# The gate and up products of a second feed-forward as seven half-size products per tile

## The chip, the cores and the metric

The kernel runs on one core of a Trainium2 chip. The metric is the device time of one execution in microseconds, the median of several runs. TensorE (PE) multiplies, VectorE (DVE), ScalarE (ACT) and GpSimd (POOL) work element by element, SyncE (SP) issues the loads; each runs its own list of instructions in order and waits for the others by semaphores.

## What is computed

One hybrid decoder layer on 512 tokens of width 1024: feed-forward, token mixing, feed-forward, each with a normalization ahead and behind and a shift, a scale and a gate from a conditioning vector. The change lies in the second feed-forward. Cut to that, the reference is

```python
def swiglu(y, w_gate, w_up, w_down):
    return (jax.nn.silu(y @ w_gate) * (y @ w_up)) @ w_down

y = rmsnorm(h, ffn2_pre_g[l]) * (1.0 + sc3) + sh3
y = swiglu(y, ffn2_w_gate[l], ffn2_w_up[l], ffn2_w_down[l])
h = h + FFN_RESIDUAL_WEIGHT * g3 * rmsnorm(y, ffn2_post_g[l])
```

with y of 512 x 1024, gate and up weights of 1024 x 2816 and down weights of 2816 x 1024, all float32.

## The kernel before

**Precision.** Every float32 operand is split into a float32r part (`hi`, a cast) and the rest (`lo`, a subtraction). A product of two operands is three matmuls in one accumulator (`mm3`, lines 110 to 113): hi by hi, then the two mixed ones. Each matmul loads its own 128 x 128 weights.

**Units.** `unit` (line 95) loads 128 x 1024 float32 (512 KB) on SP's queue into one of four raw buffers (tag `raw`), casts it on ACT (line 106) and subtracts on DVE (line 107). The results take turns in four `hi` and four `lo` buffers. A raw buffer is free again when the subtraction has read it. The names are `r_`, `h_` and `l_` for raw, hi and lo, with `b` for the second feed-forward, `a` for the first, `db` for the down weights of the second.

**Gate and up.** The 2816 columns are 22 tiles of 128. Tokens are the moving columns, so the result of a tile, 128 x 512, stands transposed in one PSUM bank for the gate and one for the up product. The first three tiles (`FF2_F`) are computed in two halves of 256 tokens, the first half of all three ahead of the second halves, because the tokens of `y` arrive in four tiles of 128 (`y_token_tile`, lines 189 to 213, with a cast and the subtraction `ylo` at line 212). The weights of f = 2 are split into a part of the tiles `hThi2` and `hTlo2` that is not yet in use. The other 19 tiles go through `up_tile`: two units, 48 matmuls of 512 columns, then `swiglu_evac` (lines 216 to 222): a sigmoid on ACT, two multiplications on DVE, the cast into `hThi2` on ACT and the subtraction into `hTlo2` on DVE.

**Rest.** Behind each of the first tiles one step of `rest` is popped: eight `ada(2, 2, j)`, each a 512 KB load and multiply-reductions on DVE (line 132) for the gate of the residual, then `gate_rows` and `gate_load`.

**Down.** `down` runs two halves of 512 output columns with 11 units each; a unit has 24 matmuls of 512 columns with `hThi2` and `hTlo2` as weights.

**Order.** The source gives the work in program order; a scheduler then sets each engine's list, and the pools of buffers decide which buffer a load takes. The `GAP` constants leave unused bytes between groups of buffers.

Of the kernel before, what the change touches and what calls it, by code (L numbers as in the profile page):

```python
# [19 lines left out]
FF = 2816  # L20
NF = FF // P
NH = 4
EPS = 1e-6
START_F = 3
GAP_W = 160
GAP_Y = 64
GAP_H = 128
GAP_M = 64
FF2_F = 3

# [2 lines left out]
def layer_kernel(ctx: ExitStack, tc: tile.TileContext, x, c, cols, gate_b,  # L33
                 ident_d, masks_d, causal_d, ada_w, wgu1, wd1, w_ft, w_vh, w_mv, w_out, wgu2, wd2, out):
    nc = tc.nc
# [19 lines left out]
    def mm_tile(name):  # L55
        return psum.tile([P, 512], F32, tag="mm", name=name)
# [4 lines left out]
    def tmp_tile(name):  # L61
        return tmp.tile([P, D], F32, tag="tmp", name=name)
# [126 lines left out]
    def y_token_tile(s, i, y, n):  # L189

        ts_ = slice(i * P, (i + 1) * P)
        for q in range(2):
# [31 lines left out]
    def k3(u):
        return tuple(v.rearrange("p (k n) -> p k n", k=KT) for v in u)
# [7 lines left out]
                    k == 0, k == KT - 1)  # L233
        swiglu_evac(f, ps[0], ps[1], hT, tag)

    def down(wd, hT, tag, s, nxt, n=NF, order=lambda f: f, pump=None, drain=None, rest=()):


        t0, ss0, later = [], [], []
        nu = n // 2  # L240
        for half in range(2):
            acc = [mm_tile(f"pd{tag}_{half}_{i}") for i in range(NT)]

            def step(u, i, v):
                for e in range(2):
                    f = order(2 * u + e)
                    mm3(acc[i], (hT[0][:, f, i * P:(i + 1) * P], hT[1][:, f, i * P:(i + 1) * P]),
                        (v[0][:, e, :], v[1][:, e, :]), u == 0 and e == 0, u == nu - 1 and e == 1)

            last = []  # L250
            for u in range(nu):
                v = unit(wd[half, u], 1024, f"d{tag}_{half}_{u}")
                v = tuple(a.rearrange("p (e n) -> p e n", e=2) for a in v)
                if rest:
                    rest.pop(0)()
                if u < nu - 4 or (drain and half == 0):
                    if drain and u == nu - 1:
                        drain()
                    for i in range(NT):
                        step(u, i, v)  # L260
                        if pump:
                            pump()
                else:
                    last.append((u, v))
            for i in range(NT):
                for n_, (u, v) in enumerate(last):
                    step(u, i, v)
                    if n_ == 0 and len(later) > 1:
                        later.pop(0)()
                if half == 0:  # L270
                    yt = small.tile([P, T], F32, tag="ysb", name=f"ysb{tag}_{i}", bufs=4)
                    ss = small.tile([P, 1], F32, tag="ssa", name=f"ssa{tag}_{i}", bufs=4)
                    nc.scalar.activation(yt, acc[i], AF.Square, accum_out=ss)
                    nc.vector.tensor_tensor(out=yt, in0=acc[i], in1=gates[s][:, 0:T], op=ALU.mult)
                    t0.append(yt)
                    ss0.append(ss)
                    continue
                post(tag, s, i, t0[i], acc[i], ss0[i], nxt is None)
                if nxt is not None:
                    nn = normed(i, nxt[0])  # L280
# [515 lines left out]


    def ffn2(y, later):
        with tc.tile_pool(name="hT2", bufs=1) as hp:
            phase(hp, "gap_h2", GAP_H)  # L800
            hT = (hp.tile([P, NF, T], F32R, name="hThi2"), hp.tile([P, NF, T], F32R, name="hTlo2"))
            us = []
            for f in range(FF2_F):
                us.append([])
                for g in range(2):
                    dst = None
                    if f == FF2_F - 1:
                        sl = slice(NF - 2 * (g + 1), NF - 2 * g)
                        dst = tuple(a[:, sl, :].rearrange("p a b -> p (a b)") for a in hT)
                    us[f].append(k3(unit(wgu2[f, g], 1024, f"b_{f}_{g}", dst)))  # L810
            ps = []
            for hf in range(2):
                sl = slice(hf * 256, (hf + 1) * 256)
                for f in range(FF2_F):
                    if hf == 0:
                        ps.append([mm_tile(f"pub_{f}_{g}") for g in range(2)])
                    for g in range(2):
                        for k in range(KT):
                            mm3(ps[f][g][:, sl], (us[f][g][0][:, k, :], us[f][g][1][:, k, :]),
                                (y[0][:, k, sl], y[1][:, k, sl]), k == 0, k == KT - 1)  # L820
                            if later and k == 3 and f == g:
                                later.pop(0)()
# [85 lines left out]
```

## Time and profile before

| what | value |
|---|---|
| median of 3 runs | 1053.97 us (1053.57 to 1054.98) |
| the profiled execution's own time | 1054.96 us |
| its span | 1053.2 us |
| mean granted clock of TensorE | 0.997 |
| gate and up, first three tiles | about 680 to 717 us |
| gate and up, 19 whole tiles | 718 to 927 us |
| down of the second feed-forward | 927 to 1045 us |

A span is the time from the first to the last instruction of the profiled execution. Busy times are sums per engine; a table by stretches shows which engine is full in which stage. A wait is named by what released it. The landing of a load is counted from its issue.

### The profile page before, as it was taken

How to read it: one execution, taken by the hardware profiler on the slowest of the kernel's cores; microseconds unless marked ns; L12 is line 12 of the kernel's file. 1: busy time of each engine (PE TensorE's matmuls, PEld its weight loads, DVE VectorE, ACT ScalarE, POOL GpSimd, SP SyncE). 2: the span in 40 equal slices, each digit the busy share in tenths (PEclk: the TensorE clock that was granted, in tenths of full speed). 3: DMA queues.
4: the chain of work that ended last, by engine and by line, in shares of the span. 5: the costliest groups of instructions: out<-in, count | busy, mean ns of one | idle time of the engine just before them, and what ended most of it. 6: DMA issues, size and time to landing. Idle time of an engine off the chain costs nothing.

```text
span 1053.2 us, 13118 instructions
## 1 busy us (share of the span) xinstructions
PE 1031.8 (98%) x4988; PEld 857.2 (81%) x4988; DVE 600.4 (57%) x1426; ACT 344.8 (33%) x496; POOL 70.7 (7%) x104
## 2 busy tenths in 40 slices
PE   6999999999999999999999999999999999999997
PEld 4778888888888878978888887898888888888886
DVE  7975465566555285387879775775543433332323
ACT  5542233222212164435343223632322222221311
POOL 1000000000000020022223131100000000000000
PEclk9999999999999999999999999999999999999999
DMA  9864445555655413333223311144454223322212
GB/s 343 279 212 152 147 153 156 164 158 165 197 180 166 149 63 126 107 124 111 100 81 100 101 61 61 44 153 146 138 111 149 92 89 101 100 99 81 100 40 80
DMA packets 42938, 136.39 MB, mean 130 GB/s; under 512 B 7670, under 2 KB 8054, under 8 KB 42876
## 3 DMA queue, kind: packets, MB, share of 16 engines
q1 hardware_dynamic: 42588, 135.41, 39.7%
q8 instruction: 39, 0.64, 0.2%
q10 hardware_dynamic: 288, 0.16, 0.1%
q14 instruction: 23, 0.19, 0.1%
HBM read 133.43 MB, written 2.12 MB: 129 GB/s over the span
## 4 chain that ended last, share of the span: by engine, by line
PE 86%; DVE 8%; issue 1%; DMA 1%; POOL 1%; ACT 1%; DVEq 0%; POOLq 0%; SPq 0%; ACTq 0%
PE pub L111 7%; PE pub L113 7%; PE pub L112 7%; PE pua L112 7%; PE pua L111 7%; PE pua L113 7%; PE pft L113 4%; PE pft L112 4%; PE pft L111 4%; PE pdb L112 4%; PE pdb L111 4%; PE pdb L113 4%; PE pda L111 4%; PE pda L113 3%; PE pda L112 3%; PE pl L576 3%
## 5 line engine op out<-in xcount | busy, mean ns | idle before, releaser
L111 PE MATMUL pub<-yhi,h_b 128*128 128x512 f32 (+1 forms) x368 | 137.8, 375 | 0.0
L113 PE MATMUL pub<-yhi,l_b 128*128 128x512 f32 (+1 forms) x368 | 137.0, 372 | 0.0
L112 PE MATMUL pub<-ylo,h_b 128*128 128x512 f32 (+1 forms) x368 | 136.0, 370 | 0.0
L111 PE MATMUL pua<-yhi,h_a 128*128 128x512 f32 x304 | 119.3, 392 | 0.7 <-DVE ta L219 0.7
L112 PE MATMUL pua<-ylo,h_a 128*128 128x512 f32 x304 | 119.8, 394 | 0.0
L113 PE MATMUL pua<-yhi,l_a 128*128 128x512 f32 x304 | 118.0, 388 | 0.0
L106 ACT CAST h_b<-r_b 128x1024 fp32r<-128x1024 f32 x42 | 44.0, 1051 | 137.8 <-issue 102.3
L107 DVE TENSOR_TENSOR l_b<-r_b,h_b 128x1024 fp32r<-128x1024 f32 x42 | 51.3, 1224 | 60.3 <-ACT h_b L106 60.3
L132 DVE CUSTOM_DVE_ANT_0 a<-a,sc 128x256 f32<-128x256 f32 x216 | 82.4, 425 | 0.0
L113 PEld LDWEIGHTS pub<-yhi,l_b 128*128 128x128 f32 x368 | 69.1, 188 | 13.4
L111 PE MATMUL pft<-yhi,h_ft 128*128 128x512 f32 x192 | 79.6, 415 | 0.0
L112 PEld LDWEIGHTS pub<-ylo,h_b 128*128 128x128 f32 x368 | 69.1, 188 | 13.0 <-DVE ylo L212 0.2
L106 ACT CAST h_a<-r_a 128x1024 fp32r<-128x1024 f32 x38 | 39.9, 1049 | 119.5 <-issue 74.9
L111 PEld LDWEIGHTS pub<-yhi,h_b 128*128 128x128 f32 x368 | 69.1, 188 | 11.3
L113 PE MATMUL pft<-yhi,l_ft 128*128 128x512 f32 x192 | 76.3, 397 | 0.0
L112 PE MATMUL pft<-ylo,h_ft 128*128 128x512 f32 x192 | 75.8, 395 | 0.0
L111 PE MATMUL pda<-h_da,hThi 128*128 128x512 f32 x176 | 69.5, 395 | 0.0
L112 PE MATMUL pdb<-l_db,hThi 128*128 128x512 f32 x176 | 69.3, 394 | 0.0
L113 PE MATMUL pda<-h_da,hTlo 128*128 128x512 f32 x176 | 69.0, 392 | 0.0
L111 PE MATMUL pdb<-h_db,hThi 128*128 128x512 f32 x176 | 69.0, 392 | 0.0
L111 PEld LDWEIGHTS pua<-yhi,h_a 128*128 128x128 f32 x304 | 57.1, 188 | 14.5 <-DVE ta L219 1.2
L112 PE MATMUL pda<-l_da,hThi 128*128 128x512 f32 x176 | 68.3, 388 | 0.0
(270 smaller groups left out, 1946.5 us busy)
## 6 DMA issues: line engine op xcount, KB each, us to landing
a<-in_ada_w_dram SPq DMA_DIRECT2D x70, 512.0 KB, 3.8
r_b<-in_wgu_dram SPq DMA_DIRECT2D x44, 512.0 KB, 3.5
r_a<-in_wgu_dram SPq DMA_DIRECT2D x38, 512.0 KB, 4.1
r_ft<-in_w_ft_dram SPq DMA_DIRECT2D x24, 512.0 KB, 3.8
r_da<-in_wd_dram SPq DMA_DIRECT2D x22, 512.0 KB, 3.4
r_db<-in_wd_dram SPq DMA_DIRECT2D x22, 512.0 KB, 3.5
r_dm<-in_w_out_dram SPq DMA_DIRECT2D x8, 512.0 KB, 4.4
r_s<-in_wgu_dram SPq DMA_DIRECT2D x12, 256.0 KB, 6.1
```

What stands on the lines that cost most here:

```text
L106: nc.scalar.copy(hi, raw)
L107: nc.vector.tensor_tensor(out=lo, in0=raw, in1=hi.bitcast(F32), op=ALU.subtract)
L111: nc.tensor.matmul(ps, lhs[0], rhs[0], start=start, stop=False)
L112: nc.tensor.matmul(ps, lhs[0], rhs[1], start=False, stop=False)
L113: nc.tensor.matmul(ps, lhs[1], rhs[0], start=False, stop=stop)
L132: nc.vector.tensor_tensor_reduce(out=raw[:, sl], in0=raw[:, sl], in1=sc[:, sl], scale=1.0, scalar=init if q == 0 else 0.0, op0=ALU.mult, o ...
L576: nc.tensor.matmul(pv[:, i, :], kk[:, sl], qq[:, sl], start=True, stop=True)
```

## The change

The 19 whole tiles are computed by seven products instead of eight, on halves: the tokens in two halves, the inner dimension in two halves, and gate and up as the two column blocks of the weights. A product has four k slices with three matmuls each, of 256 columns: 84 matmuls per tile. `Ra` holds the gate weights, `Rb` the up weights.

- Weights of the products: `plain` casts `Ra` to h1, writes l1 = -h1 on ACT, and a DMA that GpSimd issues adds the weights from DRAM onto l1. `sums` forms t3 = Rb2 - Rb1, then Rb1 - Ra1, t3 + Ra1 and its difference with Ra2 on DVE, in the raw buffers themselves; h2 and l2, h3 and l3 are the splits of these. `last` splits the second half of `Rb` (h4, l4).
- Sums of y: a hook of `y_token_tile` forms S1, S2, S3 and S4 for the third and fourth token tile, ten operations of 512 elements on DVE and three casts on ACT each; `sum4` overwrites a quarter of `y`.
- Products are chained in two banks. In A: p1, copied out (s0); p6 on top, copied (s1); p7 on top, copied (s3); p4 on top, to Silu. In B: p2 in the right half; p5, then p3 in the left half. PE's order in one period is p6, p5, p7 of a tile, p1 and p2 of the next, p4 and p3 of the first.
- Evacuation: g0 = p2 + s0, g3 = p5 + s3, g1 = p3 + s1 on DVE, two Silu on ACT, one multiplication into `hT2`, which stays float32 and whole.
- `down` splits two rows of `hT2` per unit, 22 times (one cast on ACT and one subtraction on DVE of 1024 elements). The steps of `rest` stand in `down`, two per unit for the first three. p4 and p3 of the last tile are issued there between the first steps.
- f = 2 of the first three tiles takes the usual split buffers. The first three tiles use Silu too. `GAP_W` is 192 (160), `GAP_X` of 192 stands in for `gap_h2`.

The core of the diff:

```diff
-GAP_W = 160
+GAP_W = 192
+GAP_X = 192
...
+                if split:
+                    v = (*v, split(half, u))
+                for _ in range(2 if split and u < 3 else 1):
+                    if rest:
+                        rest.pop(0)()
...
+                def plain(self):
+                    h1, l1 = self.pair("B11", "B21", wsp, 1024, ("hi", "lo"), "1")
+                    nc.scalar.copy(h1, self.Ra)
+                    nc.scalar.activation(l1, h1.bitcast(F32), AF.Copy, scale=-1.0)
+                    nc.gpsimd.dma_start(l1, wgu2[self.f, 0], accum_op=ALU.add)
+                def sums(self):
...
+                    tt(out=t3, in0=Rb[:, T:], in1=Rb[:, :T], op=ALU.subtract)
+                    tt(out=Rb[:, :T], in0=Rb[:, :T], in1=Ra[:, :T], op=ALU.subtract)
+                    tt(out=Ra[:, :T], in0=t3, in1=Ra[:, :T], op=ALU.add)
+                    tt(out=Ra[:, T:], in0=Ra[:, T:], in1=Ra[:, :T], op=ALU.subtract)
...
+                    nc.scalar.copy(h2[:, T:], t3)
+                    nc.scalar.copy(h2[:, :T], Rb[:, :T])
+                    nc.scalar.copy(h3, Ra)
+                    tt(out=l3, in0=Ra, in1=h3.bitcast(F32), op=ALU.subtract)
+                    tt(out=l2[:, :T], in0=Rb[:, :T], in1=h2[:, :T].bitcast(F32), op=ALU.subtract)
+                    tt(out=l2[:, T:], in0=t3, in1=h2[:, T:].bitcast(F32), op=ALU.subtract)
+                def last(self):
+                    h4, l4 = self.pair("B22", None, hp, T, ("X4h", "X4l"), "4")
+                    nc.scalar.copy(h4, self.Rb[:, T:])
+                    tt(out=l4, in0=self.Rb[:, T:], in1=h4.bitcast(F32), op=ALU.subtract)
...
+            for f in range(FF2_F, NF - 1):
+                w, v = W.pop(f), W[f + 1]
+                w.p6()
+                w.last()
+                w.p5()
+                v.sums()
+                w.p7()
+                if f + 2 < NF:
+                    W[f + 2] = Tile(f + 2)
+                    W[f + 2].plain()
+                v.open()
+                v.p1()
+                v.p2()
+                w.p4()
+                w.p3()
-            for f in range(FF2_F, NF):
-                up_tile(f, wgu2, y, hT, "b")
-                if rest:
-                    rest.pop(0)()
-            down(wd2, hT, "b", 2, None)
+            down(wd2, None, "b", 2, None, rest=rest, split=split, pump=pump)
```

Up to about 690 us every engine has the same list in both kernels. Three places where the lists differ follow; the first number behind a name is the tile (f), the last one only tells buffers apart.

PE at the entry, before, from the end of the first halves of f = 1 on (`pub_1_1` is its up product):

```order
L111 MATMUL pub_1_1_5686<-yhi2_5097,h_b_1_1_5599 128x256
L112 MATMUL pub_1_1_5686<-ylo2_5098,h_b_1_1_5599 128x256
L113 MATMUL pub_1_1_5686<-yhi2_5097,l_b_1_1_5600 128x256
L111 MATMUL pub_2_0_5759<-yhi2_5097,hThi2_5577 128x256
L112 MATMUL pub_2_0_5759<-ylo2_5098,hThi2_5577 128x256
L113 MATMUL pub_2_0_5759<-yhi2_5097,hTlo2_5578 128x256
L111 MATMUL pub_2_0_5759<-yhi2_5097,hThi2_5577 128x256
```

PE goes from f = 1 to the first halves of f = 2, 48 matmuls. The same place after:

```order
L112 MATMUL pub_1_1_5696<-yhi2_5097,h_b_1_1_5601 128x256
L113 MATMUL pub_1_1_5696<-ylo2_5098,h_b_1_1_5601 128x256
L114 MATMUL pub_1_1_5696<-yhi2_5097,l_b_1_1_5602 128x256
L112 MATMUL pub_0_0_5617<-yhi2_5097,h_b_0_0_5583 128x256
L112 MATMUL pub_0_1_5618<-yhi2_5097,h_b_0_1_5589 128x256
L112 MATMUL pub_1_0_5695<-yhi2_5097,h_b_1_0_5595 128x256
L112 MATMUL pub_1_1_5696<-yhi2_5097,h_b_1_1_5601 128x256
L113 MATMUL pub_0_0_5617<-ylo2_5098,h_b_0_0_5583 128x256
L114 MATMUL pub_0_0_5617<-yhi2_5097,l_b_0_0_5584 128x256
```

The second halves of f = 0 and f = 1 have moved up behind the first halves, and f = 2 comes later.

ACT in the tile stage, before, the list of one tile (sigmoid at line 218, splits at 106 and 221):

```order
L106 CAST h_b_8_0_6353<-r_b_8_0_6351 128x1024
L218 ACTIVATE tb_6_6261<-pub_6_0_6211 128x512
L106 CAST h_b_8_1_6359<-r_b_8_1_6357 128x1024
L221 CAST hThi2_5577<-tb_6_6261 128x512
L106 CAST h_b_9_0_6429<-r_b_9_0_6427 128x1024
```

Casts of units and two steps per tile alternate there. After, the stretch of tile 8 (line 904 is h1, 905 l1, 918 and 919 h2, 920 h3, 927 h4; 946 and 954 are the copies s1 and s3, 959 and 960 the two Silu):

```order
L918 CAST h2_8_6601<-t3_8_6596 128x512
L919 CAST h2_8_6601<-Rb8_6501 128x512
L904 CAST h1_9_6630<-Ra9_6626 128x1024
L960 ACTIVATE g7_6512<-g7_6512 128x256
L959 ACTIVATE g6_6386<-pA6_6383 128x256
L920 CAST h3_8_6603<-Ra8_6500 128x1024
L905 ACTIVATE l1_9_6631<-h1_9_6630 128x1024
L927 CAST h4_7_6580<-Rb7_6375 128x512
L946 COPY s12_7_6511<-pA7_6509 128x256
L954 COPY s3_7_6623<-pA7_6509 128x256
L918 CAST h2_9_6727<-t3_9_6722 128x512
```

The copy s1 (`s12_7`), which lets p7 start, stands behind h3, l1 and h4.

SP's loads of tiles 5 and 6, before:

```order
L124 DMA a_2_2_1_6115<-in_ada_w_dram 128x1024
L100 DMA r_b_5_0_6123<-in_wgu2_dram 128x1024
L100 DMA r_b_5_1_6129<-in_wgu2_dram 128x1024
L124 DMA a_2_2_2_6191<-in_ada_w_dram 128x1024
L100 DMA r_b_6_0_6199<-in_wgu2_dram 128x1024
L100 DMA r_b_6_1_6205<-in_wgu2_dram 128x1024
```

Two units and one `ada` load make a tile. After, with their waits, two loads do (GpSimd's stands in its own list):

```order
L890 DMA Ra8_6500<-in_wgu2_dram 128x1024 [waits DMAHW0_49,DVE_49]
L891 DMA Rb8_6501<-in_wgu2_dram 128x1024 [waits DMAHW2_49,DVE_49]
L890 DMA Ra9_6626<-in_wgu2_dram 128x1024 [waits DMAHW3_49,DVE_49]
L891 DMA Rb9_6627<-in_wgu2_dram 128x1024 [waits DMAHW5_49,DVE_49]
L890 DMA Ra10_6752<-in_wgu2_dram 128x1024 [waits DMAHW4_49,DVE_49]
```

Each load waits for DVE. Rb9 takes the raw buffer of Ra8 (the semaphore is that load's) and so waits for l3_8; Rb10 takes that of Rb8 and waits for l4_8; Ra9 and Ra10 follow l3_7 and l4_7. DVE's list after, from tile 9's first sum:

```order
L912 TENSOR_TENSOR t3_9_6722<-Rb9_6627 128x512
L955 TENSOR_TENSOR g7_6512<-pB7_6510,s3_7_6623 128x256
L913 TENSOR_TENSOR Rb9_6627<-Rb9_6627,Ra9_6626 128x512
L923 TENSOR_TENSOR l2_9_6728<-t3_9_6722,h2_9_6727 128x512
L914 TENSOR_TENSOR Ra9_6626<-t3_9_6722,Ra9_6626 128x512
L942 TENSOR_TENSOR g8_6638<-pB8_6636,s12_8_6637 128x256
L915 TENSOR_TENSOR Ra9_6626<-Ra9_6626 128x512
L922 TENSOR_TENSOR l2_9_6728<-Rb9_6627,h2_9_6727 128x512
L964 TENSOR_TENSOR g7_6512<-pB7_6510,s12_7_6511 128x256
L965 TENSOR_TENSOR hT2_5578<-g7_6512 128x512
L928 TENSOR_TENSOR l4_8_6707<-Rb8_6501,h4_8_6706 128x512
L921 TENSOR_TENSOR l3_9_6730<-Ra9_6626,h3_9_6729 128x1024
```

Line 921 is l3, 922 and 923 are l2, 928 is l4, 965 is the product into `hT2`. The release of Rb8's buffer (l4_8) now stands behind all sums of tile 9.

## Rows read from the trace of the kernel before

**Rows 1.** The page: busy us (share of the span) x instructions; then the chain by engine.

```profile
PE 1031.8 (98%) x4988; PEld 857.2 (81%) x4988; DVE 600.4 (57%) x1426; ACT 344.8 (33%) x496; POOL 70.7 (7%) x104
...
PE 86%; DVE 8%; issue 1%; DMA 1%; POOL 1%; ACT 1%; DVEq 0%; POOLq 0%; SPq 0%; ACTq 0%
```

**Rows 2.** Table by stretches: length, busy us (x instructions) of each engine, PEclk, DMA share, GB/s.

```profile
700.00:710.00 10.00, 10.00 (x87) 10.00 (x86) 5.41 (x10) 4.27 (x6) 0.00 (x0) 1.00 0.31 104
...
718.00:927.00 209.00, 209.00 (x915) 171.49 (x914) 91.08 (x150) 59.72 (x76) 0.00 (x0) 1.00 0.37 111
927.00:1045.00 118.00, 118.00 (x517) 96.84 (x516) 33.23 (x36) 24.20 (x34) 1.65 (x3) 1.00 0.22 76
```

**Rows 3.** Timeline of PE, 700 to 707 us: start, duration, engine, line, operation.

```profile
700.28 0.28 PE L111 MATMUL pub<-yhi,h_b 128*128 128x256 f32 x1
...
706.41 0.28 PE L112 MATMUL pub<-ylo,h_b 128*128 128x256 f32 x1
```

**Rows 4.** Waits of PE, 680 to 1046 us: total us, times, longest.

```profile
PE pst L197 <- DVE n L176: 0.4, 1, 0.4
PE pst L197 <- DVE yf L206: 0.3, 1, 0.3
```

**Rows 5.** Groups by form: count, ns min/median/max; last, the page's weight loads: busy, mean ns.

```profile
L221 ACT CAST hThi<-tb x22: 612/616/622, 707.0 to 927.0; 128x512 fp32r<-128x512 f32 x22
...
L742 DVE TENSOR_TENSOR om<-pn,rm x8: 408/425/426, 490.9 to 633.4; 128x256 f32<-128x256 f32 x8
...
L732 ACT ACTIVATE om<-pn x8: 378/386/387, 485.2 to 628.0; 128x256 f32<-128x256 f32 x8
...
L111 PEld LDWEIGHTS pua<-yhi,h_a 128*128 128x128 f32 x304 | 57.1, 188 | 14.5 <-DVE ta L219 1.2
```

**Rows 6.** Timeline of DVE, then of ACT, 740 to 746 us.

```profile
740.47 0.69 DVE L220 TENSOR_TENSOR tb<-tb,pub 128x512 f32<-128x512 f32 x1
741.07 1.23 DVE L107 TENSOR_TENSOR l_b<-r_b,h_b 128x1024 fp32r<-128x1024 f32 x1
742.20 0.69 DVE L222 TENSOR_TENSOR hTlo<-tb,hThi 128x512 fp32r<-128x512 f32 x1
...
744.78 1.05 ACT L106 CAST h_b<-r_b 128x1024 fp32r<-128x1024 f32 x1 [2.97 <-PE pub L112]
745.74 0.59 ACT L218 ACTIVATE tb<-pub 128x512 f32<-128x512 f32 x1
```

**Rows 7.** The same timelines, a handoff from ACT to DVE.

```profile
733.80 1.05 ACT L106 CAST h_b<-r_b 128x1024 fp32r<-128x1024 f32 x1 [3.39 <-PE pub L112]
...
734.88 1.23 DVE L107 TENSOR_TENSOR l_b<-r_b,h_b 128x1024 fp32r<-128x1024 f32 x1 [2.16 <-ACT h_b L106]
```

**Rows 8.** Landing: the page; 700 to 712 us; 718 to 927 us; SP's waits there.

```profile
r_b<-in_wgu_dram SPq DMA_DIRECT2D x44, 512.0 KB, 3.5
r_a<-in_wgu_dram SPq DMA_DIRECT2D x38, 512.0 KB, 4.1
...
a<-in_ada_w_dram SPq DMA_DIRECT2D x2, 512.0 KB, 5.4
r_b<-in_wgu_dram SPq DMA_DIRECT2D x2, 512.0 KB, 4.2
...
gd<-modc SPq DMA_DIRECT2D x1, 4.0 KB, 12.6
...
SPq L100 <- DVE l_b L107: 137.1, 28, 5.8
```

**Rows 9.** The entry, PE and then DVE, 694 to 699 us.

```profile
694.58 0.29 PE L111 MATMUL pub<-yhi,hThi 128*128 128x256 f32 x1
...
694.42 0.42 DVE L132 CUSTOM_DVE_ANT_0 a<-a,sc 128x256 f32<-128x256 f32 x1
...
696.37 0.68 DVE L212 TENSOR_TENSOR ylo<-yf,yhi 128x512 fp32r<-128x512 f32 x1
...
698.70 0.69 DVE L212 TENSOR_TENSOR ylo<-yf,yhi 128x512 fp32r<-128x512 f32 x1 [0.15 <-ACT yhi L211]
```

More of the change, by code (lines that the diff above doesn't have):

```diff
@@ L213, in y_token_tile @@
                                     op=ALU.subtract)
+            yfs.append(yf)
+        if hook is not None:
+            hook(i, yfs)
     def swiglu_evac(f, psg, psu, hT, tag):
@@ L234, in up_tile, with down @@
         swiglu_evac(f, ps[0], ps[1], hT, tag)
-    def down(wd, hT, tag, s, nxt, n=NF, order=lambda f: f, pump=None, drain=None, rest=()):
+    def down(wd, hT, tag, s, nxt, n=NF, order=lambda f: f, pump=None, drain=None, rest=(), split=None):
         t0, ss0, later = [], [], []
@@ L798, in ffn2, with s_tile, quarter, sums @@
     def ffn2(y, later):
+        HT = T // 2
+        K2 = KT // 2
         with tc.tile_pool(name="hT2", bufs=1) as hp:
[L800 to L810, printed above, removed]
+            tt = nc.vector.tensor_tensor
+            def s_tile(tag, at):
+                t = hp.tile([P, 3136], F32R, tag=tag, name=f"{tag}{at}")
+                return t[:, at:at + 3072]
+            Shi, Slo = (s_tile(t, 0).rearrange("p (a k t) -> p a k t", a=3, k=K2) for t in ("Shi", "Slo"))
+            hT = hp.tile([P, NF, T], F32, name="hT2")
+            phase(hp, "gap_x", GAP_X)
+            s4 = tmp_tile("s4").rearrange("p (k t) -> p k t", k=K2)
+            def quarter(a, th, kh):
+                return a[:, kh * K2:(kh + 1) * K2, th * HT:(th + 1) * HT]
+            late = []
+            def sums(i, yfs):
+                a = slice((i - 2) * P, (i - 1) * P)
+                hi1, lo1 = (v[:, 0:K2, a].bitcast(F32) for v in y)
+                hi2, lo2 = (v[:, K2:, a].bitcast(F32) for v in y)
+                r = hp.tile([P, 2, K2, P], F32, tag="X3h", name=f"sr{i}", bufs=2)
+                r3 = hp.tile([P, K2, P], F32, tag="X3l", name=f"sq{i}", bufs=2)
+                tt(out=r[:, 0], in0=yfs[0], in1=yfs[1], op=ALU.add)
+                tt(out=r3, in0=hi1, in1=yfs[0], op=ALU.subtract)
+                def rest_of():
+                    tt(out=r[:, 1], in0=r[:, 0], in1=hi1, op=ALU.subtract)
+                    nc.scalar.copy(Shi[:, 0, :, a], r[:, 0])
+                    tt(out=r[:, 1], in0=r[:, 1], in1=lo1, op=ALU.subtract)
+                    tt(out=r3, in0=r3, in1=lo1, op=ALU.add)
+                    nc.scalar.copy(Shi[:, 1, :, a], r[:, 1])
+                    nc.scalar.copy(Shi[:, 2, :, a], r3)
+                    tt(out=Slo[:, 0, :, a], in0=r[:, 0], in1=Shi[:, 0, :, a].bitcast(F32), op=ALU.subtract)
+                    tt(out=Slo[:, 1, :, a], in0=r[:, 1], in1=Shi[:, 1, :, a].bitcast(F32), op=ALU.subtract)
+                    tt(out=Slo[:, 2, :, a], in0=r3, in1=Shi[:, 2, :, a].bitcast(F32), op=ALU.subtract)
+                    tt(out=s4[:, :, a], in0=hi2, in1=r[:, 1], op=ALU.subtract)
+                    tt(out=s4[:, :, a], in0=s4[:, :, a], in1=lo2, op=ALU.add)
+                late.append(rest_of)
+            def sum4():
+                nc.scalar.copy(quarter(y[0], 1, 0), s4)
+                tt(out=quarter(y[1], 1, 0), in0=s4, in1=quarter(y[0], 1, 0).bitcast(F32), op=ALU.subtract)
+            us = [[k3(unit(wgu2[f, g], 1024, f"b_{f}_{g}")) for g in range(2)] for f in range(FF2_F)]
@@ new lines, in ffn2, with product @@
+            ya = {"A11": tuple(quarter(a, 0, 0) for a in y), "A12": tuple(quarter(a, 0, 1) for a in y),
+                  "S4": tuple(quarter(a, 1, 0) for a in y), "A22": tuple(quarter(a, 1, 1) for a in y)}
+            for n_, nm in enumerate(("S1", "S2", "S3")):
+                ya[nm] = (Shi[:, n_], Slo[:, n_])
+            def product(ps, w, x, start):
+                for k in range(K2):
+                    c = slice(k * P, (k + 1) * P)
+                    mm3(ps, (w[0][:, c], w[1][:, c]), (x[0][:, k, :], x[1][:, k, :]), start and k == 0, k == K2 - 1,
+                        skip_group_check=True)
@@ new lines, in ffn2 @@
+            W = {f: Tile(f) for f in (FF2_F, FF2_F + 1)}
+            W[FF2_F].plain()
+            W[FF2_F].sums()
+            sum4()
+            W[FF2_F + 1].plain()
+            W[FF2_F].open()
+            W[FF2_F].p1()
+            W[FF2_F].p2()
+            for f in range(FF2_F, NF - 1):
[13 more added lines that the diff above has]
+                w.p3()
@@ new lines, in ffn2, with pump, split @@
+            w = W[NF - 1]
+            w.p6()
+            w.last()
+            w.p5()
+            w.p7()
+            todo = [w.p4, w.p3]
+            def pump():
+                if todo:
+                    todo.pop(0)()
+            hd = [s_tile(t, 32).rearrange("p (c a b) -> p c a b", c=3, a=2) for t in ("Shi", "Slo")]
+            def split(half, u):
+                c = (half * (NF // 2) + u + 3) % 5
+                if c < 3:
+                    hi, lo = hd[0][:, c], hd[1][:, c]
+                else:
+                    hi, lo = (hp.tile([P, 1024], F32R, tag=t, name=f"hs{t}{half}_{u}", bufs=2)
+                              .rearrange("p (a b) -> p a b", a=2) for t in ("X3h", "X3l"))
+                src = hT[:, 2 * u:2 * u + 2, :]
+                nc.scalar.copy(hi, src)
+                tt(out=lo, in0=src, in1=hi.bitcast(F32), op=ALU.subtract)
+                return hi, lo
```

81 lines of the change are left out of this document (68 added, 13 removed).

## The prediction

> **What bounds the kernel now.** I read the page's busy times and its chain first: TensorE is busy 98% of the span and carries 86% of the chain [rows 1]. An average over stages says little, so the table by stretches comes next: from 718 to 927 us, where the 19 whole tiles of the second feed-forward run, PE is busy for all of the 209.00 us with 915 matmuls, while DVE works 91.08 and ACT 59.72 us [rows 2]. PE's waits from 680 to 1046 us come to 0.7 us [rows 4]. So this stage is bound by the number of matmuls times their pitch, and nothing else ends it. The pitch: 209.00/915 = 0.2284 us for 512 columns; the 256-column matmuls that start at 700.28 and 706.41 are 52 apart, 0.1179 us each [rows 3], and the stretch from 700 to 710 agrees (87 in 10 us) [rows 2]. Half the columns cost 51.6%, not 50%. The granted clock is 1.00 in all these stretches, the 2.4 GHz level, and PE has no gap in which it could fall.
>
> **The change part by part.**
>
> Matmuls. A tile had 48 matmuls of 512 columns, 48 x 0.2284 = 10.96 us; it gets seven products of 12 with 256 columns, 84 x 0.1179 = 9.90 us. If PE stayed the only limit, 19 tiles would give 19 x 1.06 = 20.1 us. I weigh here a rule of the Trainium skill, "TensorE: Matmul & The Clock Gate", section "The mechanism": a weight load overlaps a running matmul only when the row group differs. Every matmul here loads new weights on the full array; by that rule a load would stand beside each matmul. The trace disagrees: 87 matmuls and 86 loads of 10.00 us together lie in the same 10 us [rows 2].
>
> Engine work per tile. By the starts of neighbours on DVE, an operation on 512 elements advances the queue 0.60 us and one on 1024 elements 1.13 us; ACT's 1024-element cast 0.96 us [rows 6], each about 0.09 us less than its duration. A tile's DVE list is then eight of 512 (4.8), l3 (1.13) and three of 256 columns from PSUM (425 ns alone, so 0.34 each): 6.95 us. ACT has h1, l1, h3 (2.88), three casts of 512 (617 ns alone, 0.53 each: 1.59) and five of 256 columns (385 ns alone, 0.30: 1.5): 5.97 us [rows 5]. Both stay under 9.90, so neither engine is the bound by its amount.
>
> The ring. What can bind is the loop through the four raw buffers. SP's load of Rb of one tile waits for l3 of the tile before, and the next tile's for l4 of that same tile; between load and release stands a chain in which every link waits for the one before, since DVE and ACT take their lists in order. For an even tile: t3, Rb, Ra and an l2 (4 x 0.60), g0 (0.34), Ra' (0.69), h3 on ACT (1.05), l3 (1.23): 5.71 us. For an odd one: t3, g3, Rb (0.60 + 0.34 + 0.69), then on ACT h2, h1, a Silu, l1, a Silu, h3 (0.53 + 0.96 + 0.30 + 0.96 + 0.30 + 0.96 = 4.01) and h4 (0.62), then l4 (0.69): 6.95 us. A handoff between engines costs 0.03 us (a cast that ends at 734.85, its DVE partner at 734.88) [rows 7]. Mean with handoffs: 6.5 us. A tile's period is therefore the larger of 9.90 and 6.5 + L, with L the time from issue to landing of Rb; PE shows it as a wait of p7 for ACT's copy s1, which stands behind h4 in ACT's list.
>
> L is not seen for this mixture, so by the nearest rows: 3.5 us for the loads of this stage before, two and an ada per tile and well spread; 4.1 for the first feed-forward, which loads three times 512 KB per tile as the changed stage does (Ra, Rb and the accumulating transfer); 4.2 and 5.4 where 710 us draws near and loads queue behind each other [rows 8]. I take 4.1, the row with the same three transfers per tile: 10.6 us. With 3.5 the ring gives 10.0, with 5.4 it gives 11.9. The trace's 137.1 us of SP's waits [rows 8] were covered by buffers loaded a tile ahead; here Ra has that lead and Rb has not.
>
> The accumulating transfer. GpSimd issues it after l1 and p1's third matmul wants it. POOL is idle in the stage before [rows 2], so its queue holds nothing else. l1's buffer comes free with p2 two tiles earlier, so it has two periods, less p1 and p2 (2.8) and h1, l1 and what ACT does between (3.8): hidden up to 2 x 9.9 - 6.6 = 13.2 us. Nearest rows: 3.5 to 5.4 for plain loads, 12.6 for the slowest small one, the 4 KB write of the gate rows [rows 8]. I take it as hidden.
>
> Entry. Before, PE bridged the wait for the last token tile with first-half matmuls of f = 2, from 694.58 to 700.28 us [rows 3, 9]; there f = 2 wrote its weights into the hT tiles. Now f = 2 waits for split buffers that f = 0 frees, so PE goes straight to the second halves at 694.6. Their first four k slices need the ylo that starts at 696.37 and lasts 0.68, the others the one at 698.70 [rows 9]: PE waits until 697.05 (2.4 us), works 12 x 0.118 = 1.4 us to 698.46, waits until 699.39 (0.9). That is 3.3 us if DVE keeps its times. Between them DVE loses ada pieces (0.42 us each; about four here) [rows 9] and gains sums of 512 elements (0.60; about two), which nearly cancel. Then comes the first tile's chain (its l1 behind a Silu, the table load of Silu, its l3), hidden by the three short tiles. I take 3.5, with 1.5 (DVE earlier) and 7 (first chain exposed) as ends.
>
> Down. Splitting hT there adds 22 x (1.05 ACT + 1.23 DVE), and the eight moved ada steps about 1.8 each on DVE. DVE goes from 33.23 to some 75 and ACT from 24.20 to some 47 of 118 us [rows 2, 6], beside PE, which has the ring of split buffers as cover. I take nothing; 1.5 if the first units, with two ada loads each, come late. The moved buffer addresses (the GAP constants) have no row to price them: nothing, with 1 us either way, about the spread of the runs.
>
> Sum. Before: 19 x 10.96 = 208.3. After: the first and last tile have no ring behind them, 17 x 10.6 + 2 x 9.9 + 3.5 = 203.5. Difference -4.8 us; against the profiled execution (1054.96) 1050.2, and against the median of 1053.97, which lies 1.0 below it, **1049 us**.
>
> **The rivals.**
>
> *The ring doesn't bind.* If Rb lands in 3.5 us or less, the median of this stage now [rows 8], the period is 9.9 to 10.0: 19 x 9.9 + 3.5 = 191.6, so -16.7 and 1037; with 10.0 1039. For it: DMA engines are 37% busy there [rows 2]. Against: the accumulating transfer is issued when Rb's load is.
>
> *Rb always meets the other transfers: slower.* ACT does l1 right after h3, so GpSimd's transfer starts about as l3 frees the buffer for Rb, and the next Ra follows when l4 is done. Where loads met before, they took 4.2 and 5.4 [rows 8]. With 4.8, their middle, the period is 11.3: 17 x 11.3 + 19.8 + 3.5 = 215.4, +7.1, 1061; with 5.4, 225.6, 1071. It decides from a period of 10.9, L = 4.4 us. The Trainium skill, "DMA: Bandwidth & Descriptors", section "Issuing engines are not separate DMA queues", speaks for this: transfers of all issuers run on the same 16 engines and interleave. The 5.4 us beside other loads agrees.
>
> *The accumulating transfer is slow.* Beyond 13.2 us PE waits at p1's third matmul; the period is (D + 6.6)/2. 16 us give 11.3, 1061; 20 give 13.3, 1095. Nothing shows one so long. The Trainium skill, same page, section "Anatomy of one DMA - SWDGE (gpsimd) path", fits a plain transfer from GpSimd as 2.0 us plus its bytes over 436 KB per us, 3.2 us as an estimate for 512 KB; no run here shows it yet.
>
> *Weight loads don't overlap.* Then a tile costs 84 x 0.188 [rows 5] = 15.8 us at least in loads, 19 x (15.8 - 10.96) = +92, 1146. The 87 in 10 us [rows 2] speak against it.
>
> **How the numbers follow.** The ring with L near 4.1: 0.43; by its own ends (3.8 to 4.5) 1044 to 1056. The ring not binding: 0.27. Rb always colliding: 0.22. A slow accumulating transfer: 0.06. Weight loads or something unseen: 0.02. A difference under 0.2% (2.1 us) is about what this measurement can't tell from none. Below 1051.9: the 0.27 and 0.28 of the first, 0.55. Within: 0.12 of the first. Above 1056.1: 0.03 of the first, 0.22, 0.06 and 0.02, 0.33. The range takes in the unbound ring, 1036, and the collision to L = 5.1, 1066; a slow accumulating transfer beyond that and the top of the collision are left out.
>
> **What would show it.** Matmuls of 256 columns at 0.118 us, 84 to a tile. PE's waits: some 0.7 us per tile at p7 for ACT (s1) if the ring binds; none if it doesn't; at p1 for a DMA if the accumulating transfer is late. SP's wait for l3 and l4 shortly before each Rb, and Rb's landing near 4.1 us. Around 694 to 700 us a wait of PE for DVE's ylo of about 3 us. I am wrong if PE waits for DVE or ACT work that is not behind Rb, or if down shows waits for the split hT.

## The result

| | median us | runs | ratio to before, 95% interval |
|---|---|---|---|
| before | 1053.77 | 1053.47 to 1054.98 | |
| changed | 1084.57 | 1081.87 to 1084.89 | 1.0284 (1.0266 to 1.0303) |

The change is slower by 31 us. The forecast was 1049 with a range from 1036 to 1066. The span of the profiled execution is 1082.9 us (before 1053.2).

From the page of the changed kernel: busy times, the chain by engine, then issues with KB and median us to landing.

```profile
PE 1025.5 (95%) x5672; PEld 882.5 (81%) x5672; DVE 692.9 (64%) x1596; ACT 427.6 (39%) x656; POOL 86.5 (8%) x123
...
PE 17%; DMA 9%; ACT 4%; DVE 4%; issue 1%; DVEq 0%; POOLq 0%; ACTq 0%
...
Ra<-in_wgu_dram SPq DMA_DIRECT2D x19, 512.0 KB, 5.9
Rb<-in_wgu_dram SPq DMA_DIRECT2D x19, 512.0 KB, 5.5
l<-in_wgu_dram POOLq DMA_DIRECT2D x19, 512.0 KB, 7.2
```

The shares of this chain add up to 36% only: the profile could follow it back to 688.3 us and no further, so its 17% for PE can't be set beside the 86% of [rows 1]. By its pieces from 720 to 950 us, DMA has 93 of the 230 us, ACT 45, PE 44 and DVE 35; in the kernel before PE has all of them. The loads that took 3.5 us [rows 8] take 5.9 and 5.5 us at the median, the accumulating one 7.2. PE's waits from 720 to 950 us (total, times, longest), where the kernel before had none [rows 4]:

```profile
PE pA L112 <- ACT s L946: 28.2, 18, 3.6
PE pB L112 <- DVE g L942: 2.8, 4, 1.1
PE pA L114 <- DMA l<-in_wgu_dram: 1.0, 1, 1.0
PE pA L114 <- DVE l L921: 0.9, 1, 0.9
```

With two of under 0.4 us they sum to 33 us, 28.2 of it for the copy s1 ahead of p7 (line 946). The stretch from 720 to 920 us, columns as in [rows 2]:

```profile
720.00:920.00 200.00, 169.44 (x1324) 164.78 (x1323) 117.36 (x191) 100.41 (x176) 14.95 (x17) 0.95 0.52 130
```

PE lies idle for 30.6 of 200 us, and the mean granted clock is 0.95. PE's timeline shows the two levels, with the idle time and its releaser in brackets:

```profile
748.43 0.28 PE L114 MATMUL pB<-Shi,l 128*128 128x256 f32 x1
752.29 0.58 PE L112 MATMUL pA<-Shi,h 128*128 128x256 f32 x1 [3.59 <-ACT s L946]
752.68 0.41 PE L113 MATMUL pA<-Slo,h 128*128 128x256 f32 x1
752.89 0.41 PE L114 MATMUL pA<-Shi,l 128*128 128x256 f32 x1
...
757.95 0.28 PE L114 MATMUL pB<-yhi,l 128*128 128x256 f32 x1
758.07 0.28 PE L112 MATMUL pB<-yhi,h 128*128 128x256 f32 x1
```

Ahead of the wait the starts are 0.11 to 0.12 us apart, behind 3.59 us of waiting 0.21, the 1.2 GHz level, until 757.95; then 0.12 again. A mean of 0.95 means a tenth of the time at half speed: 20 us of these 200 do the work of 10.

**Where the 30 us lie.** The first product of a whole tile starts at 718.2 us (before: first matmul 717.29), down's first matmul starts at 951.3 (926.0), its last one at 1076.0 (1046.7). The tile stage without the two products that moved into down lasts 233.1 us, where 1572 matmuls of 0.118 are 185. The 48 us above that are 33 of waits, some 10 lost at the lower clock (all of it between 720 and 920 us), and a rest of 4. With those two products (2.8) the stage has 235.9 us where it had 208.7: 27.2 us more. The entry adds 0.9 us, down 1.2.

**The loop.** Issues on GpSimd and SP (start, duration), then DVE's t3 and l4 and ACT's h1 on the same scale; the last line is the sum of h1's waits for Ra from 765.8 to 927.1 us (total, times, longest):

```profile
802.42 0.88 POOL L906 DMA_DIRECT2D l<-in_wgu_dram  x1 [13.36 <-ACT l L905]
...
790.22 0.33 SPq L891 DMA_DIRECT2D Rb<-in_wgu_dram  x1
802.34 0.33 SPq L891 DMA_DIRECT2D Rb<-in_wgu_dram  x1
803.28 0.33 SPq L890 DMA_DIRECT2D Ra<-in_wgu_dram  x1
...
796.26 0.69 DVE L912 TENSOR_TENSOR t<-Rb 128x512 f32<-128x512 f32 x1 [3.91 <-DMA Rb<-in_wgu_dram]
...
806.60 0.69 DVE L912 TENSOR_TENSOR t<-Rb 128x512 f32<-128x512 f32 x1 [2.75 <-DMA Rb<-in_wgu_dram]
...
802.57 0.68 DVE L928 TENSOR_TENSOR l<-Rb,h 128x512 fp32r<-128x512 f32 x1
...
814.70 0.69 DVE L928 TENSOR_TENSOR l<-Rb,h 128x512 fp32r<-128x512 f32 x1 [0.76 <-ACT h L927]
...
810.64 1.05 ACT L904 CAST h<-Ra 128x1024 fp32r<-128x1024 f32 x1 [1.75 <-DMA Ra<-in_wgu_dram]
...
ACT h L904 <- DMA Ra<-in_wgu_dram: 11.2, 6, 2.5
```

Rb of tile 10 is issued at 790.22, behind l4 of tile 8, and t3 waits for it until 796.26: 6.0 us. From there DVE and ACT need 7.0 us until l4 of tile 9 (802.57 + 0.68) lets SP issue Ra of tile 12 at 803.28. It lands 7.3 us later: ACT's h1 starts at 810.64. Behind h1 in ACT's list stand l1, h3 and h4, then l4 at 814.70, and the next Rb at 815.42. So 6.0 + 7.0 + 7.4 + 4.8 = 25.2 us for two tiles; from the Rb at 765.84 to the one at 927.06, 13 tiles, the mean period is 12.4 us. The issues also show why loads are late: 802.34, 802.42 and 803.28 are three transfers of 512 KB within 1 us.

The Rb issued at 802.34 landed sooner: t3 starts at 806.60, 4.3 us later. Over these 13 tiles the two kinds take turns, 3.9 to 4.4 us and 5.3 to 6.0 from the issue of Rb to the start of t3, 5.0 on average. The page's median of 5.5 leaves out landings that the profile could not place, in this stretch every second one.

The profile's chain takes PE's way through the second part of this loop: from s1 at 802.8 its matmuls run until 811.48 and release a Silu; Ra's way through h1 ends at 811.59. Here the two are even, so taking only one of them away need not shorten the loop by all of it.

### The profile page after: what moved, and what is told of

It reads as the page before. It is cut to its first block, busy times and chain, and to the rows that moved or that the text cites. A ratio compares the mean times of both kernels' runs of the same rounds, so it can differ in the third digit from the quotient of the medians.

```text
span 1082.9 us, 14911 instructions
## 1 busy us (share of the span) xinstructions
PE 1025.5 (95%) x5672; PEld 882.5 (81%) x5672; DVE 692.9 (64%) x1596; ACT 427.6 (39%) x656; POOL 86.5 (8%) x123
## 3 DMA queue, kind: packets, MB, share of 16 engines
q0 software_dynamic: 2736, 9.96, 5.3%
## 5 line engine op out<-in xcount | busy, mean ns | idle before, releaser
L112 PE MATMUL pA<-Shi,h 128*128 128x256 f32 x152 | 46.8, 308 | 28.4 <-ACT s L946 28.2
L114 PEld LDWEIGHTS pua<-yhi,l_a 128*128 128x128 f32 x304 | 57.1, 188 | 13.4
L113 PEld LDWEIGHTS pua<-ylo,h_a 128*128 128x128 f32 x304 | 57.1, 188 | 12.7
L108 DVE TENSOR_TENSOR l_a<-r_a,h_a 128x1024 fp32r<-128x1024 f32 x38 | 46.5, 1223 | 23.1 <-ACT h_a L107 23.0
L112 PEld LDWEIGHTS pA<-Shi,h 128*128 128x128 f32 x152 | 30.5, 201 | 32.2 <-ACT s L946 31.9
L107 ACT CAST h_da<-r_da 128x1024 fp32r<-128x1024 f32 x22 | 23.1, 1048 | 77.8 <-PE pda L114 58.5
L108 DVE TENSOR_TENSOR l_da<-r_da,h_da 128x1024 fp32r<-128x1024 f32 x22 | 26.9, 1225 | 34.4 <-ACT h_da L107 34.1
L112 PE MATMUL pA<-yhi,h 128*128 128x256 f32 x152 | 44.5, 293 | 1.7 <-ACT s L954 1.7
L114 PE MATMUL pA<-Shi,l 128*128 128x256 f32 x152 | 44.8, 295 | 0.9 <-DVE l L921 0.9
L114 PE MATMUL pA<-yhi,l 128*128 128x256 f32 x152 | 44.0, 289 | 1.0 <-DMA l<-in_wgu_dram 1.0
```

Source lines behind the costliest of these rows:

```text
L114: nc.tensor.matmul(ps, lhs[1], rhs[0], start=False, stop=stop, **kw)
```

## Experiments

The ratios are to the kernel before, run on the same chip.

### Is it the transfers?

**e1.** Without the accumulating transfer.

```diff
-                    nc.gpsimd.dma_start(l1, wgu2[self.f, 0], accum_op=ALU.add)
```

> The changed kernel without the accumulating DMA: l1 stays -h1, so a third of the tile's transfers and their landing are left out, and the output is not the reference's. Theory A (ring through the raw buffers, lengthened because three 512 KB transfers of a tile are issued within about 2 us and share the DMA engines): Ra and Rb land in 4.2 to 4.7 instead of 5.5 to 5.9 us, the loop of two tiles falls from some 25 (6.0 + 7.0 + 7.1 + 4.8) to some 21 us, PE's wait for the copy s1 falls from 28 to under 12 us, time 1045 to 1055. Theory B (the lists of ACT and DVE themselves are the bound, loads only look late): within 4 us of 1084.6.

Measured 1043.1 us, 0.990 (0.988 to 0.991). Landings and PE's wait for s1:

```profile
Ra<-in_wgu_dram SPq DMA_DIRECT2D x19, 512.0 KB, 4.3
Rb<-in_wgu_dram SPq DMA_DIRECT2D x19, 512.0 KB, 3.5
...
PE pA L112 <- ACT s L945: 4.6, 8, 1.4
```

The time is 2 us below theory A's range, and the wait is 4.6 us instead of 28.2. Theory B falls. The scheduler shifted a few instructions of the lists here, so the next run is the cleaner one.

**e2.** The same bytes without the addition; every list of every engine is that of the changed kernel.

```diff
-                    nc.gpsimd.dma_start(l1, wgu2[self.f, 0], accum_op=ALU.add)
+                    nc.gpsimd.dma_start(l1, wgu2[self.f, 0])
```

> The accumulating DMA made a plain one from the same queue with the same bytes (the output is not the reference's: l1 holds the weights). If the addition in the transfer is what slows the loads, as e1: 1045 to 1055. If it is the bytes in flight at the same time (theory A), within 8 us of 1084.6, Ra and Rb landing at 5 us or more. Theory B: within 4 us of 1084.6.

Measured 1060.0 us, 1.006 (1.005 to 1.008): 24.6 us less than with the addition. Its queue's line (packets, MB, share of the span of 16 engines) for the changed kernel, then for e2, and e2's landings:

```profile
q0 software_dynamic: 2736, 9.96, 5.3%
...
q0 software_dynamic: 2736, 9.96, 2.9%
...
Ra<-in_wgu_dram SPq DMA_DIRECT2D x19, 512.0 KB, 4.8
Rb<-in_wgu_dram SPq DMA_DIRECT2D x19, 512.0 KB, 4.3
```

Neither expectation was met: the time lies between the two ranges. A packet took its engine 0.053 x 16 x 1082.9 / 2736 = 0.34 us on average with the addition and 0.029 x 16 x 1057.5 / 2736 = 0.18 us without. The loads of SP beside it land 1.1 and 1.2 us earlier when it only copies. So of the 41 us between the changed kernel and e1, some 25 are the addition and some 17 the bytes. The forecast's row, 4.1 us for three plain loads per tile [rows 8], fits e2 (4.3 to 4.8), not a stage in which one of the three adds.

**e5.** l1 on DVE, no third transfer.

```diff
-                    nc.scalar.activation(l1, h1.bitcast(F32), AF.Copy, scale=-1.0)
-                    nc.gpsimd.dma_start(l1, wgu2[self.f, 0], accum_op=ALU.add)
+                    tt(out=l1, in0=self.Ra, in1=h1.bitcast(F32), op=ALU.subtract)
```

> l1 = Ra - h1 by one subtraction on DVE in place of ACT's -h1 and the accumulating DMA (the first form of the change without its transfer). DVE gains 1.13 us per tile, ACT loses 0.96, two transfers are left. Theory A: Ra and Rb land in 4.2 to 4.7 us, loop some 21 us for two tiles, 1045 to 1056. Theory B: DVE's list is longer, so 1085 to 1105.

Measured 1046.6 us, 0.993 (0.992 to 0.995), faster than the kernel before. The scheduler set the lists of ACT and DVE anew. A piece of the chain (start, us):

```profile
794.46 1.14 DVE l L905
```

DVE's l1 (line 905) now stands in the loop itself, beside a landing of Rb of 3.6 us at the median; the period is 10.4 us.

**e12 and e14.** The transfer as it is, but later. In both the lists of ACT, DVE, SP and PE are those of the changed kernel.

```diff
+                    for n_ in range(2):
+                        nc.gpsimd.tensor_tensor(out=dl, in0=l1[:, :T].bitcast(F32), in1=l1[:, T:].bitcast(F32), op=ALU.add)
                     nc.gpsimd.dma_start(l1, wgu2[self.f, 0], accum_op=ALU.add)
```

> The changed kernel with every list of ACT, DVE, SP and PE as it is; only GpSimd runs two additions of 512 elements (into a spare buffer, reading l1) ahead of each accumulating DMA, so that this transfer starts some 2 to 3 us later. Theory A3 (it matters that the accumulating transfer is in flight while Rb and Ra land): Rb, issued within 1 us of it now, lands in some 4 us instead of 5.5, Ra still meets it: loop of two tiles 4 + 7.0 + 6.5 + 4.8 = 22.3, 11.2 per tile, 1055 to 1068. Theory A1 without A3 (only the order on ACT matters): within 5 us of 1084.6. If the addition itself is late: PE waits for the DMA at p1, above 1090.

Measured 1083.2 us, 1.027 (1.025 to 1.029). Rb's median landing fell to 4.1 us and the time did not. But GpSimd's additions slowed DVE. GpSimd's pair, then DVE's l4 beside it:

```profile
788.82 2.99 POOL L908 TENSOR_TENSOR dl<-l 128x512 f32<-128x512 f32 x2 [5.71 <-ACT l L905]
...
790.58 1.78 DVE L931 TENSOR_TENSOR l<-Rb,h 128x512 fp32r<-128x512 f32 x1
```

l4 takes 1.78 us here and 1.43 at the median instead of 0.69, so this run tells nothing of the theories. The Trainium skill, "GPSIMD Engine Reference", section "Specifications", states that GpSimd's SBUF interfaces are shared with VectorE, with contention where a VectorE instruction has two SBUF inputs; this row, with two SBUF inputs, agrees.

e14 has five additions of one element per partition in their place.

> As the late addition, but the delay on GpSimd is five additions of one element per partition (some 0.55 us each) instead of two of 512, so that DVE is not slowed beside them; every list of ACT, DVE, SP and PE is that of the changed kernel. If the meeting of the transfers is what lengthens the loop (theory A3), Rb and Ra land in some 4 and 5 to 6 us and the time falls to 1058 to 1072. If it is the order on ACT that lets Ra's landing into the loop, whichever transfer is late (theory A1), the landing only moves from Rb to Ra: 1078 to 1088.

Measured 1071.6 us, 1.017 (1.015 to 1.019). Landings, then the pieces of the chain (start, us):

```profile
Ra<-in_wgu_dram SPq DMA_DIRECT2D x19, 512.0 KB, 5.8
Rb<-in_wgu_dram SPq DMA_DIRECT2D x19, 512.0 KB, 4.2
...
786.51 7.93 DMA Ra<-in_wgu_dram
...
799.31 5.44 DMA Ra<-in_wgu_dram
...
810.75 7.01 DMA Ra<-in_wgu_dram
```

Rb lands in 4.2 us, Ra in 5.8, and 13 us are gained: the time is at the upper end of theory A3's range. But in the chain Ra now stands in place of Rb, 5.4 to 7.9 us each time, as theory A1 had said. Both have a part: the meeting of the transfers, and the list that lets Ra's landing count.

### Is it the order?

**e6.** h1 and l1 of the next tile stand behind h3, h4 and s1 on ACT. The scheduler moved DVE's list with it.

```diff
+                    self.h3i = nc.scalar.copy(h3, Ra)
+                    self.h4i = nc.scalar.copy(h4, self.Rb[:, T:])
+                    self.s1i = nc.scalar.copy(self.s[:, 1], self.A[:, :HT])
...
-                    W[f + 2].plain()
+                    with tc.issue_after(v.h3i.ins), tc.issue_after(w.h4i.ins), tc.issue_after(w.s1i.ins):
+                        W[f + 2].plain()
```

> The changed kernel with one order fixed on ACT: the next tile's h1 and l1 stand behind this tile's h3, h4 and s1, so that the landing of Ra is no longer waited for inside the loop. Theory A1 (in-order lists put both Rb's and Ra's landing into the loop of two tiles: 6.0 + 7.0 + 7.3 + 4.8 = 25.1): the loop loses the part of Ra that is not covered and becomes two times (5.5 + some 6.2), 11.7 per tile instead of 12.5: 1065 to 1076. Theory A2 (only the transfers' length matters, not who waits for which): 1080 to 1088.

Measured 1046.3 us, 0.992 (0.991 to 0.994), with the accumulating transfer as it was. Landings and PE's wait for s1:

```profile
Ra<-in_wgu_dram SPq DMA_DIRECT2D x19, 512.0 KB, 4.8
Rb<-in_wgu_dram SPq DMA_DIRECT2D x19, 512.0 KB, 3.5
l<-in_wgu_dram POOLq DMA_DIRECT2D x19, 512.0 KB, 6.1
...
PE pA L112 <- ACT s L946: 2.8, 5, 1.0
```

The gain of 38 us is twice what was expected. h1's wait for Ra no longer delays h3, h4 and s1, and since l1 now comes later, the accumulating transfer starts some 2 us behind Rb: Rb lands in 3.5 us although the third transfer still takes 6.1. The period falls to 10.2 us (Rb at 799.62 and 809.85). So this run takes two things away at once, the wait for Ra and a part of Rb's landing.

**e3.** A fifth raw buffer.

```diff
-    wraw = ctx.enter_context(tc.tile_pool(name="wraw", bufs=4))
+    wraw = ctx.enter_context(tc.tile_pool(name="wraw", bufs=5))
-            raw = wsp.tile([P, 1088], F32, tag=park, name=f"r_{name}")[:, :n]
+            raw = wsp.tile([P, 1040], F32, tag=park, name=f"r_{name}")[:, :n]
```

(and 1040 for 1088 in the other split buffers)

> A fifth raw buffer (room for it comes from split buffers cut from 1088 to 1040 columns). Theory A: each load can be issued one load earlier, about half a tile, so Rb's landing of 5.5 us is covered by that lead; PE's wait for s1 falls below 8 us and the granted clock returns to 1.00: 1040 to 1050. Theory B: no change, 1080 to 1088.

Measured 1071.4 us, 1.016 (1.014 to 1.017), 13 us better and not 35 to 45. SP's issues of Rb, then DVE's t3 of the next tile and the l4 and l3 behind it:

```profile
785.29 0.33 SPq L891 DMA_DIRECT2D Rb<-in_wgu_dram  x1
797.57 0.33 SPq L891 DMA_DIRECT2D Rb<-in_wgu_dram  x1
...
791.53 0.69 DVE L912 TENSOR_TENSOR t<-Rb 128x512 f32<-128x512 f32 x1 [3.91 <-DMA Rb<-in_wgu_dram]
...
795.72 0.68 DVE L928 TENSOR_TENSOR l<-Rb,h 128x512 fp32r<-128x512 f32 x1
796.32 1.22 DVE L921 TENSOR_TENSOR l<-Ra,h 128x1024 fp32r<-128x1024 f32 x1
```

Rb is issued at 785.29, t3 starts when it has landed, 791.53; behind it in DVE's list stand the other sums, then l4 and l3, and when l3 has ended SP issues the next Rb, at 797.57. The loop of one tile, 12.3 us here and 11.8 on average, still goes through a landing, and the chain runs through DVE at this place and not through h1: the additional lead was spent by the list in which the next tile's t3 stands ahead of the l4 and l3 that free buffers.

**e7.** Both, e6 and e3 together.

> The same order and a fifth raw buffer, the accumulating DMA kept. Theory A1: with the order fixed the fifth buffer really gives a lead, Rb's landing of 5.5 us is followed only by t3, Rb, a g and l3 (some 3 us) before the next issue, below the 9.9 of PE: the ring no longer binds, 1037 to 1047. Theory A2: little below the fifth buffer alone, 1062 to 1072.

Measured 1054.1 us over ten runs, 1048.9 to 1056.8, 0.999 (0.998 to 1.001): 7.8 us slower than e6, a miss. The chain (start, us):

```profile
790.56 4.98 DMA Rb<-in_wgu_dram
...
798.74 1.23 DVE l L921
...
800.30 0.61 DVE l L928
...
800.92 5.79 DMA Rb<-in_wgu_dram
```

Rb is issued behind l4 and takes 5.0 to 5.8 us again, then t3, g0, a Silu, h3, l3 and l4 follow: 10.4 us here, 10.5 per tile on average. I had taken l3 as its release and 3 us of work; with five buffers the scheduler wrote other lists, in which the next tile's t3 stands ahead of both.

**e9 and e10.** l1 on DVE with the order of e6, with four and with five raw buffers.

> l1 by a DVE subtraction and the fixed order on ACT, with four raw buffers. If the fifth buffer is needed to cover the landing: loop 3.6 + some 7 = 10.6 per tile, 1043 to 1050. If order and traffic were all: 1036 to 1040, as with five buffers.

> l1 by a DVE subtraction, the fixed order and the fifth raw buffer together. Theory A1: no landing is left in the loop, PE's waits in the tile stage fall below 3 us and only the entry is lost: 1036 to 1043. If DVE's longer list (some 8.1 us per tile) or the entry bounds it instead: 1044 to 1050.

e9: 1045.3 us, 0.992 (0.990 to 0.994). e10: 1037.2 us, 0.984 (0.982 to 0.985), the best of all, faster than both kernels. The stretch 720 to 900 us of e10, and all of PE's waits in it:

```profile
720.00:900.00 180.00, 179.44 (x1554) 179.04 (x1554) 162.28 (x274) 101.38 (x187) 0.00 (x0) 1.00 0.35 120
...
PE pA L114 <- DVE l L920: 0.5, 1, 0.5
```

1554 matmuls in 179.44 us are 0.1155 each, and 0.5 us of waiting is left: PE bounds the stage again, at 9.7 us per tile (84 x 0.1155).

### Other terms

**e8.** 20 matmuls of no use ahead of p7, to hold the clock up.

```diff
+                junk_ps = tr_tile(f"fill{f}")
+                for n_ in range(20):
+                    nc.tensor.matmul(junk_ps[:, :HT], w.w["T3"][0][:, :P], ya["S3"][0][:, 0, :], start=n_ == 0,
+                                     stop=n_ == 19)
```

> The changed kernel with 20 idle matmuls of 256 columns per tile into a spare bank ahead of p7, where PE waits for s1 (18 tiles x 20 x 0.118 = 42 us more PE work, the rest unchanged). If the tile stage is bound by the ring alone, PE's slack of some 2 us per tile takes them: time within 6 us of 1084.6. If the granted clock (0.83 to 1.00 there) costs time on the path, the clock returns to 1.00 and the time falls by up to 14 us. If PE is the bound, 1110 or more.

Measured 1107.2 us, 1.050 (1.048 to 1.052), with the clock at 1.00; of its four executions one took 2702 us, which nothing here explains. But the scheduler answered with other lists. Pieces of the chain (start, us):

```profile
793.30 4.99 DMA Rb<-in_wgu_dram
...
803.41 1.04 ACT l L905
...
804.72 0.94 ACT h L920
...
806.93 5.00 DMA Rb<-in_wgu_dram
```

l1 and h3 both stand behind a Silu here, and from one Rb's issue to the next it is 13.6 us. The loop itself grew, so what the clock alone costs stays open.

**e13.** The kernel before with the moved addresses.

```diff
-GAP_W = 160
+GAP_W = 192
```

> The kernel before with GAP_W at 192 instead of 160, nothing else: the moved addresses, which the prediction priced at nothing. Within 1.5 us of 1054; a change beyond 2 us would be part of the measured 30.

Measured 1054.1 us, 1.000 (0.999 to 1.001): nothing, as priced. The addresses that only the changed kernel has were not tried alone.

## Why the prediction was wrong

**What held.** The matmuls: 84 per tile at 0.1155 to 0.118 us; where the loop no longer binds, e10 shows 9.7 us per tile for the 9.9 that was worked out. The Trainium skill's rule on weight loads, "TensorE: Matmul & The Clock Gate", section "The mechanism", would have given 92 us more as the forecast read it; 1554 matmuls and as many loads in 180 us of e10 contradict it again. DVE and ACT are no bound by their amount. The ring through the raw buffers is the bound, PE shows it at p7 as a wait for s1, as written; the hidden accumulating transfer itself cost PE one wait of 1.0 us. Down cost 1.2 us (0 to 1.5), and no wait of PE there is for the split hT; the moved addresses of `GAP_W` cost nothing (e13). The formula of the ring held too, 6.5 us of work and the landing, as the table below shows.

**What failed first: L, the landing of Rb.** The step took 4.1 us from the row of three loads per tile. That row has three transfers which are all plain and issued 1.3 to 5.6 us apart (137 to 159 us of the kernel before); here they start within 1 us, and one adds. 5.0 us were measured, 0.9 more per tile; the forecast's own formula then gives 6.5 + 5.0 = 11.5 us, and 17 x 11.5 + 19.8 + 3.5 = 218.8, 10.5 us slower, 1064. This was the rival "Rb always meets the other transfers", which had 0.22 and a price of 1061 to 1071. Its mechanism is what happened (e2, e14), and the rows of 4.2 and 5.4 us, the ones with loads that met, should have been taken: their middle, 4.8, stood in the forecast.

**What failed second: "Ra has that lead and Rb has not".** SP issues Ra about 1 us behind Rb (802.34 and 803.28), and ACT's list has the next tile's h1 ahead of this tile's h3 and h4. The forecast's chain of an odd tile has this h1 with its work of 0.96 us and with no wait. The wait was 11.2 us in 13 tiles, 0.9 per tile, some 15 us over the stage. Both facts were in the lists ahead of the forecast. By the formula the first failure alone would have left the time inside the range, if narrowly; the second took it out. Together they are 17 x 1.8 = 31 of the 36 us by which the forecast was short; most of the rest lies in the first periods of the stage, 13.4 to 15.3 us from 723 to 766 us.

How well the two together account for the period, in us, means over the loads of Rb of tiles 8 to 20 (L from the issue of Rb to the start of t3, the last term from ACT's waits for Ra at h1):

| run | L | h1's wait per tile | 6.5 + both | period measured |
|---|---|---|---|---|
| changed | 5.0 | 0.9 | 12.4 | 12.4 |
| e1, no third transfer | 3.6 | 0.1 | 10.2 | 10.2 |
| e2, third transfer plain | 4.1 | 0.3 | 10.9 | 11.0 |
| e14, third transfer later | 4.0 | 1.1 | 11.6 | 11.8 |
| e6, order on ACT | 3.6 | 0 | 10.1 | 10.3 |

The lists of e1 and e6 differ a little from those for which the 6.5 was worked out. e14 leaves the wait for Ra in and gains by L alone; the 38 us of e6 are not the order's alone, since by the formula more of them come from L (1.4 per tile) than from the wait (0.9).

**The clock.** "PE has no gap in which it could fall" was true of the kernel before. The forecast gave PE a wait of 0.7 us in every tile and kept the clock at 1.00; at such waits that was no error: in e1 and e3, whose waits are up to 1.4 and 1.7 us, the granted clock from 720 to 920 us is 1.00. Behind the longer waits of the changed kernel PE worked 20 us at the 1.2 GHz level, some 10 us of its own account. The period above adds up without a term for it, but in one place (752.3 to 762.0 us) the chain does run through such matmuls. How much of the 10 us the time would get back at the full clock is open.

**The sum by its terms.** By what PE did. Waits: forecast 17 x 0.7 = 12, measured 33. Clock: 0, some 10. Entry: 3.5, measured 0.9, below its low end of 1.5, which hides 2.6 us of the miss; PE waited 1.0 us for `yhi` and `ylo` at 694.7 instead of 3.3; with the ada steps gone from DVE's list there, the last `ylo` starts at 696.13 instead of 698.70 [rows 9]. Down: 0, measured 1.2. Rest of the stage: 0, 4. Together 21 + 10 - 2.6 + 1.2 + 4 = 34 us more than forecast; 1049 + 34 = 1083, measured 1084.6.

The removals are not additive, which speaks for one loop: without the third transfer 1046.6 (e5), with the order 1046.3 (e6), with both 1045.3 (e9). Each cuts the same loop to about the same length, some 10.3 to 10.5 us per tile; with both of them a fifth buffer brings the rest (e10). A fifth buffer without the third transfer but in the old order was not tried.

## What to carry to other kernels

Before a loop is priced with a transfer's usual landing, list what else is issued within a microsecond of it, and take the row with as many transfers in flight, an accumulating one counted double, as its packets were here. Trace every instruction of the loop that reads a load, and give each its wait and not only its work. A buffer or a lead is worth only what the in-order list behind it lets through: look for the instruction that waits for a later load and stands ahead of the one that frees a buffer, and reorder before buffers are added. If a forecast gives PE a wait per tile, look for a row with waits as long and read its granted clock.

## What the runs showed of the hardware

- A packet of the transfer that adds into SBUF took its DMA engine 0.34 us on average, one of a copy of the same bytes 0.18 us (changed kernel, e2), and the loads beside the adding one land about 1.1 us later.
- GpSimd additions of 512 elements stretch a DVE subtraction of 512 elements from 0.69 to 1.43 us at the median and 1.78 at most (e12); with additions of one element per partition it stayed at 0.68 (e14).
- After 3.6 us without matmuls PE worked at the 1.2 GHz level for 5.7 us (752.29 to 757.95), and its mean granted clock over 720 to 920 us was 0.95; with waits of up to 1.7 us it was 1.00 (e3).
